# A two-layer RWKV-7 and differential-attention block: the parts of a recurrence step written first, its portions of other work behind them

## The chip, the cores and the metric

The kernel runs on one core of a Trainium2 chip. The time is device time in microseconds, the median of several runs; single runs of the kernel before lie between 2425.6 and 2431.77 us. The engines of the core are TensorE (PE), VectorE (DVE), ScalarE (ACT), GpSimd (POOL) and SyncE (SP), which here only issues DMAs. Each works through its own queue of instructions in order and waits at semaphores for the others.

## The reference

One sequence of 256 context tokens and 512 latent tokens (width 1024) goes through two layers. Each layer modulates a normalized input (adaLN), projects it, and mixes it in two ways: differential attention, and an RWKV-7 recurrence over 8 heads of 64, forward and backward. Then come the output projection and a squared-ReLU MLP. What matters here is the recurrence, and what is done with its result:

```python
def step(state, inp):
    r_t, w_t, k_t, v_t, kk_t, b_t = inp
    sa = jnp.einsum("bhvk,bhk->bhv", state, kk_t)
    state = (state * w_t[:, :, None, :] - sa[..., :, None] * b_t[:, :, None, :]
             + v_t[..., :, None] * k_t[:, :, None, :])
    y = jnp.einsum("bhvk,bhk->bhv", state, r_t)
    return state, y

for d, reverse in enumerate((False, True)):
    state_c, yc = wkv_scan(state0, rc, dec_c, km_c, vc, kkc, b_c, reverse)   # context first
    _, yl = wkv_scan(state_c, r, dec, km, v, kk, bb, reverse)                # then latents
    y_lat, y_ctx = y_lat + yl, y_ctx + yc
out = rwkv_finish(y_lat, ...)   # norm per head, bonus, gate
```

The modulation vectors are `silu(c) @ ada_w[l] + ada_b[l]`, six of width 1024 for each layer. Outputs of the context are not needed in the last layer.

## The kernel before

The recurrence works in chunks. A tile has 128 tokens, two chunks of 64; 6 tiles make the 768 tokens, in both directions d = 0 and 1 (d = 1 takes the tiles in another order). For each tile and direction **preparation** (`preps`, lines 962 to 1070) computes scaled keys and the products of keys with keys, G, in two halves of four heads. That needs a loading part (`prep_a`) and four more pieces (`prep_b`), so 5 portions for a half, 20 for both directions, and one more that reports the tile as ready. Then **inversion** (`inv`): blocks of G go to DRAM in another layout (`relay`, line 1086), come back (W and N, lines 1115 and 1116), are inverted by 30 pairs of instructions (`eliminate`, lines 1100 and 1102; on DVE from tile 2 on, on POOL for tiles 0 and 1), are stored (1123, 1127) and loaded back (1132, 1137), and `merge` joins the blocks with 64 small matmuls (1152 to 1162) and two copies (1164, 1165). An inversion has 11 portions.

A **step** (n, j) is chunk j of the n-th tile in both directions. It is a generator that yields after each part: X for d = 0 and 1 (lines 1186, 1189; evacuated by 1192), U (1198, 1201), the state (1210, 1213, 1215, 1218; left out in the last step) and Y (1226, 1236 or 1239; left out for the context in the last layer). That makes 8 parts, or 6. U of step (n, 0) is the first to need the merged G of tile n. After a tile's last Y, **finish** (lines 1244 to 1296, 3 portions) normalizes, gates and stores it for the output projection. **adaLN** (`ada_half`, line 265) streams its weights through three buffers of 512 KB on the SP queue; four pieces a step are drawn, and their loads are queued behind the last uv load of the step (`self.gate`, line 1176).

The order of instructions in each engine's queue is set when the kernel is built. A planner runs all instructions against its own estimate of their durations. When an engine is free in this estimate, it gets, of the instructions whose inputs the estimate holds ready, the one that is written earliest in the program. So the place in the program is a rank and not a fixed position. What the planner has laid down is the order on the chip, also where the real times differ from the estimate.

The loop that the change touches is in `rest()`. `work` holds finish portions, `ada` the adaLN pieces, `prepg` the preparation, `invs` the inversions; each call draws one portion.

```python
for _ in step(n, j):
    work(1)
    if nst == 0:
        with tc.issue_after(self.gate.ins):
            ada(ADA[l])
    nst += 1
    for _ in range(4):
        if n < 4 and n + 2 not in ready:
            next(prepg)
            ...
    invs(1)
```

Of the kernel before, what the change touches and what calls it, by code (L numbers as in the profile page):

```python
# [26 lines left out]
ADA = [4, 4]  # L27
# [137 lines left out]
class K:  # L165
# [760 lines left out]
    def recurrence(self, l, last, es, side):  # L926

        nc, tc, I, dr = self.nc, self.tc, self.I, self.dr
# [146 lines left out]
        def prep_until(n):  # L1075
            while n not in ready:
                next(prepg)
# [66 lines left out]
        def merge(n):  # L1144
            TT = tts.pop(n)
            Gs = [sets[(n, d)][2].rearrange("s u h t -> s (u h) t") for d in range(2)]
            a, e = slice(0, 32), slice(32, 64)
            get = late.get("pg", bank)
            zps = get([64, 16, 32])
            Z = iv.tile([64, 16, 32], F32, name=self.n("Z"), tag="Z")  # L1150
            for u in range(16):
                nc.tensor.matmul(zps[e, u, :], Gs[0][a, u, 32:64], TT[a, u, :],
                                 start=True, stop=True, skip_group_check=True)
                nc.tensor.matmul(zps[a, u, :], Gs[1][e, u, 0:32], TT[e, u, :],
                                 start=True, stop=True, skip_group_check=True)

            nc.scalar.copy(Z.rearrange("p u (i r) -> p u r i", r=2), zps.rearrange("p u (r i) -> p u r i", r=2))
            nps = get([64, 16, 32])
            for u in range(16):
                nc.tensor.matmul(nps[a, u, :], Z[e, u, :], Gs[0][e, u, 32:64],  # L1160
                                 start=True, stop=True, skip_group_check=True)
                nc.tensor.matmul(nps[e, u, :], Z[a, u, :], Gs[1][a, u, 0:32],
                                 start=True, stop=True, skip_group_check=True)
            nc.vector.tensor_copy(Gs[0][a, :, 32:64], nps[a])
            nc.scalar.copy(Gs[1][e, :, 0:32], nps[e])
# [138 lines left out]
        def rest():  # L1304
            nonlocal uvp, fp, px, us, xsd
            side.drain()
            setp.extend([self.pool(es, "sets", 1) for _ in range(2)])
            uvp = self.pool(es, "uvp", 2)
            xsd = [uvp.tile([128, 512], F32, name=self.n("xs"), bufs=1) for _ in range(2)]
            for x in xsd:  # L1310
                nc.gpsimd.memset(x[64:128], 0.0)
            fp = self.pool(es, "fp", 1)
            pg, pa, *px = (self.pool(es, "pg", 1, PSUM) for _ in range(4))
            late["pg"] = lambda shape: pg.tile(shape, F32, name=self.n("pg"), tag="g")
            us = self.pool(es, "pus", 1, PSUM).tile([128, 2, 4, 64], F32, name=self.n("us"))
            pms.append(self.pool(es, "pmr", 1, PSUM))
            ada = Fill()
            kinds = (("mix", "rows"), ("mlp", "cols"), ("mlp", "rows"))
            for kd, how in kinds:
                ada.add((self.ada_rows if how == "rows" else self.ada_cols)(l, kd, pa, "a"))  # L1320
            if l == 0:
                ada.add(self.ada_cols(1, "mix", pa, "a"))
            work = Fill()
            prep_until(1)
            invs = Fill()
            for n in range(6):
                if n == 0:
                    merge(0)
                    merge(1)
                for j in range(2):  # L1330
                    nst = 0
                    for _ in step(n, j):
                        work(1)
                        if nst == 0:
                            with tc.issue_after(self.gate.ins):
                                ada(ADA[l])
                        nst += 1

                        for _ in range(4):
                            if n < 4 and n + 2 not in ready:  # L1340
                                next(prepg)
                                if n + 2 in ready:

                                    invs.add(inv(n + 2))
                        invs(1)
                if n == 4:
                    invs.drain()
                while done:
                    work.add(finish(done.pop(0)))
            work.drain()  # L1350
            ada.drain()
            if l == self.dbg.get("layer", 0) and "orT" in self.dbg:
                for j in range(4):
                    nc.sync.dma_start(self.dbg["orT"][j], self.od[j])
# [385 lines left out]
```

## Time and profile before

| | us |
|---|---|
| median of 3 runs | 2428.95 |
| the profiled execution | 2426.55 |
| its span, first to last instruction | 2424.8 |
| PE busy | 2250.5 (93%) |
| DVE busy | 1518.5 (63%) |
| ACT busy | 1174.4 (48%) |
| POOL busy | 803.6 (33%) |

The busy time of PE is that of matmuls, which overlap in its pipeline. The granted clock is the share of full speed that PE is given. A busy share over the whole span is a mean over stages with different limits; the recurrence stands in the span twice, once for each layer, at about 490 to 760 us and 1757 to 2010 us.

### The profile page before, as it was taken

How to read it: one execution, taken by the hardware profiler on the slowest of the kernel's cores; microseconds unless marked ns; L12 is line 12 of the kernel's file. 1: busy time of each engine (PE TensorE's matmuls, PEld its weight loads, DVE VectorE, ACT ScalarE, POOL GpSimd, SP SyncE). 2: the span in 40 equal slices, each digit the busy share in tenths (PEclk: the TensorE clock that was granted, in tenths of full speed). 3: DMA queues.
4: the chain of work that ended last, by engine and by line, in shares of the span. 5: the costliest groups of instructions: out<-in, count | busy, mean ns of one | idle time of the engine just before them, and what ended most of it. 6: DMA issues, size and time to landing. Idle time of an engine off the chain costs nothing.

```text
span 2424.8 us, 43738 instructions
## 1 busy us (share of the span) xinstructions
PE 2250.5 (93%) x17150; PEld 1903.9 (79%) x17150; DVE 1518.5 (63%) x2629; ACT 1174.4 (48%) x2393; POOL 803.6 (33%) x1048
## 2 busy tenths in 40 slices
PE   6999998899988999999999999999879988999997
PEld 5887887787777988888888887778767877788886
DVE  5456458647755675555556736665856575778784
ACT  4345547545534544333344435555735544555552
POOL 1212324832212343333330422323562121553530
PEclk9999999779998999999999999999879988999999
DMA  7543445377577521111112344454567664423230
GB/s 275 157 131 87 122 126 134 81 207 186 148 190 221 196 92 60 64 61 62 61 63 85 136 137 133 115 144 110 115 171 198 153 181 161 165 88 121 86 114 35
DMA packets 291630, 313.67 MB, mean 129 GB/s; under 512 B 139680, under 2 KB 220896, under 8 KB 291424
## 3 DMA queue, kind: packets, MB, share of 16 engines
q1 hardware_dynamic: 280320, 284.66, 38.8%
q0 software_dynamic: 10240, 23.08, 5.0%
q8 instruction: 135, 2.21, 0.4%
q10 hardware_dynamic: 864, 3.15, 0.3%
q14 instruction: 71, 0.58, 0.1%
HBM read 257.04 MB, written 53.77 MB: 128 GB/s over the span
## 4 chain that ended last, share of the span: by engine, by line
PE 66%; DVE 10%; DMA 8%; issue 5%; POOL 4%; ACT 4%; SPq 2%; ACTq 0%; POOLq 0%; DVEq 0%
PE pf L351 32%; PE pu L351 16%; PE po L351 4%; DMA raw<-in_ada_w 2%; PE po L832 2%; PE pb L1046 2%; PE sc L795 1%; DVE wl L1500 1%; POOL pr L1100 1%; POOL W L1102 1%; PE X L1189 1%; DVE nm L797 1%; PE X L1226 1%; PE adar L265 1%; PE ptr L815 1%
## 5 line engine op out<-in xcount | busy, mean ns | idle before, releaser
L1500 DVE TENSOR_TENSOR wl<-raw,wh 128x1024 fp32r<-128x1024 f32 x170 | 255.8, 1507 | 125.0 <-ACT wh L1499 124.2
L351 PE MATMUL pf<-hl,wh 128*128 128x512 f32 (+1 forms) x832 | 282.1, 342 | 0.0
L351 PE MATMUL pf<-hh,wh 128*128 128x512 f32 (+1 forms) x832 | 280.5, 342 | 0.6 <-ACT hh L397 0.6
L351 PE MATMUL pf<-hh,wl 128*128 128x512 f32 (+1 forms) x832 | 275.7, 342 | 0.0
L1499 ACT ACTIVATE wh<-raw 128x1024 fp32r<-128x1024 f32 x170 | 179.2, 1058 | 161.5 <-PE pf L351 143.9
L351 PE MATMUL pf<-wh,fah 128*128 128x512 f32 x570 | 224.5, 396 | 13.2 <-DVE fu L1633 7.2
L351 PE MATMUL pu<-hh,wh 128*128 128x512 f32 (+1 forms) x632 | 223.7, 354 | 4.8 <-DVE t L557 1.7
L351 PE MATMUL pf<-wl,fah 128*128 128x512 f32 x570 | 223.9, 394 | 0.7 <-DVE wl L1500 0.7
L351 PE MATMUL pf<-wh,fal 128*128 128x512 f32 x570 | 221.4, 394 | 1.8 <-DVE fal L1600 1.8
L351 PE MATMUL pu<-hh,wl 128*128 128x512 f32 (+1 forms) x632 | 218.6, 346 | 4.0 <-DVE wl L340 4.0
L351 PE MATMUL pu<-hl,wh 128*128 128x512 f32 (+1 forms) x632 | 218.0, 345 | 0.0
L797 DVE TENSOR_REDUCE nm<-sc 128x1 f32<-128x768 f32 (+1 forms) x160 | 132.5, 841 | 79.3 <-PE sc L795 78.5
L351 PEld LDWEIGHTS pf<-hl,wh 128*128 128x128 f32 x832 | 156.6, 188 | 20.0 <-DVE hl L399 0.2
L351 PEld LDWEIGHTS pf<-hh,wl 128*128 128x128 f32 x832 | 156.1, 188 | 20.0
L351 PEld LDWEIGHTS pf<-hh,wh 128*128 128x128 f32 x832 | 155.3, 188 | 20.4 <-ACT hh L397 0.8
L799 ACT ACTIVATE e<-sc,nm 128x768 f32<-128x768 f32 (+1 forms) x160 | 130.7, 821 | 53.9 <-DVE nm L797 44.3
L321 POOL TENSOR_TENSOR rs<-ms,pw 128x1 f32<-128x1 f32 (+2 forms) x60 | 56.7, 948 | 271.2 <-DVE ms L319 270.5
L351 PEld LDWEIGHTS pu<-hh,wh 128*128 128x128 f32 x632 | 121.2, 192 | 23.4 <-DVE t L557 2.4
L351 PEld LDWEIGHTS pf<-wh,fah 128*128 128x128 f32 x570 | 107.2, 188 | 40.6 <-ACT fah L1599 13.6
L1633 DVE TENSOR_TENSOR acc<-pf,acc 128x512 f32<-128x512 f32 x155 | 104.2, 682 | 53.9 <-PE pf L351 53.3
L351 PEld LDWEIGHTS pu<-hh,wl 128*128 128x128 f32 x632 | 121.0, 192 | 19.0 <-DVE wl L340 4.8
L351 PEld LDWEIGHTS pu<-hl,wh 128*128 128x128 f32 x632 | 121.1, 192 | 14.3 <-issue 1.7
(262 smaller groups left out, 5607.1 us busy)
## 6 DMA issues: line engine op xcount, KB each, us to landing
raw<-in_w_ff SPq DMA_DIRECT2D x128, 512.0 KB, 3.7
raw<-in_ada_w SPq DMA_DIRECT2D x96, 512.0 KB, 6.5
raw<-in_w_in SPq DMA_DIRECT2D x52, 512.0 KB, 4.0
ld<-zd SPq DMA_DIRECT2D x40, 384.0 KB, 5.5
ks<-qd POOLq DMA_DIRECT2D x64, 192.0 KB, 5.4
zd<-zr SPq DMA_DIRECT2D x22, 384.0 KB
raw<-in_w_out SPq DMA_DIRECT2D x16, 512.0 KB, 5.9
qs<-qd POOLq DMA_DIRECT2D x32, 192.0 KB, 5.9
```

The source lines that it names most:

```text
L265: nc.tensor.matmul(acc[32 * g:32 * g + 32, :], self.sc[:, 2 * kp + k, :], raw[:, k, g * 128:g * 128 + 128], start=(kp + k == 0), stop=(kp ...
L321: nc.gpsimd.tensor_tensor(r, m, self.pw1.to_broadcast([128, cols]), ALU.pow)
L351: nc.tensor.matmul(out, a, b, start=(start and i == 0 and j == 0), stop=(i == n - 1 and j == 2), skip_group_check=not start)
L795: nc.tensor.matmul(sc[:, k0:k1], qs[:, br, tk], ks[:, br, k0:k1], start=True, stop=True)
L797: nc.vector.tensor_reduce(nm, sc, AX.X, ALU.max, negate=True)
L799: nc.scalar.activation(ee, sc, AF.Exp, bias=nm, accum_out=ls[:, br:br + 1])
L815: nc.tensor.transpose(pt[:, (k - k0) * 128:(k - k0) * 128 + 128], e[0][:, k * 128:k * 128 + 128], self.ident)
L832: nc.tensor.matmul(po, pT[:, k * 128:k * 128 + 128], vn[:, k, h * 64:h * 64 + 64], start=(k == 0), stop=(k == nk - 1))
L1046: nc.tensor.matmul(pgt[:, u, 0:nn], BK[hs, u, :], KR[hs, 2 * pp + u, 0:nn], start=True, stop=True, skip_group_check=True)
L1499: nc.scalar.activation(hi, src, AF.Copy)
L1500: nc.vector.tensor_tensor(lo, src, hi.bitcast(F32), sub)
L1633: nc.vector.tensor_tensor(d, p, d, add)
```

## The change

The step's generator is run to its end first, and its parts are counted. Then adaLN's pieces are drawn, and after them, once for every part, a finish portion, three portions of preparation instead of four, and an inversion portion. No instruction is added or taken away.

```diff
                 for j in range(2):
-                    nst = 0
-                    for _ in step(n, j):
+                    parts = sum(1 for _ in step(n, j))
+                    with tc.issue_after(self.gate.ins):
+                        ada(ADA[l])
+                    for _ in range(parts):
                         work(1)
-                        if nst == 0:
-                            with tc.issue_after(self.gate.ins):
-                                ada(ADA[l])
-                        nst += 1
-
-                        for _ in range(4):
+                        for _ in range(3):
                             if n < 4 and n + 2 not in ready:
                                 next(prepg)
                                 if n + 2 in ready:
                                     invs.add(inv(n + 2))
                         invs(1)
```

## Rows read from the trace of the kernel before

**Rows 1.** The page: busy time of PE, and its granted clock in 40 slices.

```profile
PE 2250.5 (93%) x17150; PEld 1903.9 (79%) x17150; DVE 1518.5 (63%) x2629; ACT 1174.4 (48%) x2393; POOL 803.6 (33%) x1048
...
PEclk9999999779998999999999999999879988999999
```

**Rows 2.** Windows: stretch, length, busy per engine (instructions), PEclk, DMA share, GB/s.

```profile
492.90:760.00 267.10, 245.18 (x3484) 198.03 (x3483) 170.84 (x462) 128.05 (x301) 65.50 (x112) 0.87 0.76 197
...
1757.00:2010.00 253.00, 227.12 (x3271) 188.85 (x3269) 159.81 (x439) 123.12 (x287) 77.11 (x171) 0.87 0.67 173
1757.00:1803.00 46.00, 33.65 (x464) 27.39 (x461) 19.66 (x45) 15.49 (x38) 31.34 (x82) 0.70 0.63 158
1847.00:1888.00 41.00, 39.66 (x520) 32.33 (x518) 31.53 (x99) 24.95 (x65) 9.19 (x22) 1.00 0.70 197
```

**Rows 3.** Groups by line, PE, 492.9 to 760: count, busy us, mean ns, idle before.

```profile
L265 PE MATMUL adar<-raw,sc 128*32 128x128 f32 x768 | 40.1, 301 | 14.4 <-DMA raw<-in_ada_w 13.6 <-DVE W L1102 0.6
```

**Rows 4.** Waits of PE in 490:740, then 1757:2010: us, times, longest.

```profile
PE adar L265 <- DMA raw<-in_ada_w: 13.6, 8, 2.8
...
PE us L1210 <- DVE st L1213: 8.5, 3, 5.2
```

**Rows 5.** Timeline of PE around step (4,1): start, us, instruction, [idle before].

```profile
702.10 1.39 PE L1186 MATMUL X<-uv,S 64*128 64x64 f32 x16
...
705.70 2.05 PE L1189 MATMUL X<-sbd,S 128*128 128x128 f32 x16
...
710.13 0.64 PE L265 MATMUL adar<-raw,sc 128*32 128x128 f32 x16 [1.71 <-DMA raw<-in_ada_w]
...
710.96 0.69 PE L1198 MATMUL us<-xs,S 128*64 128x64 f32 x16
711.48 0.98 PE L1226 MATMUL X<-uv,S 128*64 128x64 f32 x14
...
712.91 0.69 PE L1210 MATMUL us<-uv,S 128*64 128x64 f32 x16
```

**Rows 6.** Timeline of ACT, steps (4,1) and (5,0): first evacuation of X.

```profile
707.10 0.59 ACT L1192 ACTIVATE xs<-X 64x512 f32<-64x512 f32 x1
...
719.64 0.59 ACT L1192 ACTIVATE xs<-X 64x512 f32<-64x512 f32 x1 [0.27 <-PE X L1189]
```

**Rows 7.** Timeline of PE, DVE and ACT, 726 to 736: merge and U of (5,0).

```profile
726.84 0.22 PE L1162 MATMUL pg<-S,Z 32*32 32x32 f32 x2
...
732.08 2.08 PE L1281 MATMUL pb<-S,cst 128*128 128x512 f32 x2 [1.46 <-POOL S L1279]
...
735.09 1.12 PE L1198 MATMUL us<-xs,S 128*64 128x64 f32 x16
...
728.15 0.69 DVE L1282 TENSOR_TENSOR S<-pb,S 128x512 f32<-128x512 f32 x1 [5.25 <-DMA S<-zd]
...
729.36 0.67 DVE L1164 COPY S<-pg 32x512 f32<-32x512 f32 x1
...
730.66 1.50 ACT L1291 ACTIVATE S<-pb,pc 128x128 f32<-128x128 f32 x4 [2.53 <-PE pb L1288]
732.18 0.58 ACT L1165 COPY S<-pg 32x512 f32<-32x512 f32 x1
```

**Rows 8.** Timeline of PE, layer 1, ahead of U of (5,0).

```profile
1968.93 2.07 PE L1281 MATMUL pb<-S,cst 128*128 128x512 f32 x2
...
1978.32 2.07 PE L1281 MATMUL pb<-S,cst 128*128 128x512 f32 x2
...
1985.46 1.12 PE L1198 MATMUL us<-xs,S 128*64 128x64 f32 x16
```

**Rows 9.** Timeline of the SP queue, layer 1: the last load of N, tile 5.

```profile
1934.09 0.67 SPq L1116 DMA_DIRECT2D N<-da  x1
```

**Rows 10.** Timeline of DVE and PE, layer 1, step (0,0): eliminations and state.

```profile
1795.71 0.40 DVE L1100 TENSOR_TENSOR pr<-W,N 128x30 f32<-128x30 f32 x1 [3.15 <-DMA N<-da]
...
1800.09 1.12 PE L1210 MATMUL us<-uv,S 128*64 128x64 f32 x16 [5.20 <-DVE st L1213]
```

## The prediction

> **What bounds the kernel now.** I read the page first. Its engine line shows TensorE (PE) busy for 93% of the span; its slices show two regions in which the granted clock falls to 0.7 or 0.8 of full speed, slices 8 to 13 and 29 to 34 [rows 1]. The recurrence of layer 0 lies in the first, that of layer 1 in the second. The busy time by windows then gives each stage: 492.9 to 760 us and 1757 to 2010 us, together 520.1 us, with PE busy for 245.18 and 227.12 us, so idle for 21.9 and 25.9 us, and a mean granted clock of 0.87 in both [rows 2]. The clock has two levels, 2.4 and 1.2 GHz (shares 1.0 and 0.5); a mean of 0.87 is 26% of the time at the lower one, some 69 and 66 us, in which half as much gets done. All that a new order inside the recurrence can win is therefore about 48 us of idle time and about 67 us of clock. PE's work itself stays.
>
> Next, what PE does there. The groups by line show that the largest single line in layer 0 is not one of the step's products but the adaLN products, 768 with 40.1 us busy, laid between the parts [rows 3]. The list of waits says what ends PE's idle time: in layer 0 the adaLN weights, 13.6 us in 8 waits, the longest 2.8 us; in layer 1 an addition of the state on DVE, 8.5 us in 3 waits [rows 4]. A portion that waits holds the chain behind it, since each engine works in order.
>
> How long a step must be: in the full-clock rows around step (4,1) the products of one direction take 1.39 us (line 1186), half of 2.05 (1189), 0.69 (1198), 0.98 for 14 of 16, so 1.1 (1226), and 0.69 (1210): 4.9 us, 9.8 for both [rows 5]. From the first evacuation of X in this step, at 707.10, to that of the next, at 719.64, are 12.5 us [rows 6], with no preparation left to do. The 12 steps of layer 0 fill 267.1 us, 22 each. The difference is the portions' work, idle time and clock.
>
> **The change part by part.** No instruction is added or removed. What changes is the order of writing, which the planner reads as rank: of two instructions that its estimate holds ready, the earlier written one gets the engine. (a) All 6 to 8 parts of a step now outrank every portion written in that step; between steps the ranks stay. (b) Preparation goes on by 3 portions a turn instead of 4. A tile pair needs 21 (4 units of 1 + 4, and one more). With 4 a turn it is through in turn 6 of 8, with 3 in turn 7, so the inversion is begun one turn later; in layer 1, whose first four steps have 6 parts, 6 x 3 = 18 is short of 21, and it ends in the first turn of the next step. (c) adaLN, written behind the first part until now, is written behind the last. SP and POOL get the same instructions: the loads of adaLN stay behind the step's last uv load, and relay, N, W and finish loads are ranked behind both uv loads in either order.
>
> First term, adaLN. Its waits are real losses, because the step's products are queued behind them: at 710 us PE idles for 1.71 us before an adaLN product, and U of the second direction starts only at 710.96 [rows 5]. Written behind the step, an adaLN product is taken only where the planner holds no product of the step ready, hence later against its load. Bounds: nothing, and all of 13.6 us [rows 4]. The longest wait is 2.8 us; yielding to the X products of both directions alone, 2 x (1.39 + 1.03) = 4.8 us [rows 5], is more than that. I take three quarters, 10.2 us, and not all, because the first gap that the estimate leaves can still come before the load.
>
> Second term, the finish portions in step (5,0). In layer 0 the last two merge products start at 726.84 and end at 727.06, and U starts at 735.09. Between them the chain needs only the two copies of the merge, 0.67 us on DVE and 0.58 on ACT. But the DVE copy (729.36) stands behind a finish product that a load holds until 728.15; the ACT copy (732.18) behind four finish evacuations; U behind finish's matmuls of 2.08 us [rows 7]. 735.09 - 727.06 - 1.25 = 6.8 us are lost. Bounds 0 and 6.8; I take half, 3.4, since a finish instruction that the estimate holds ready while the merge is not goes first in either order. In layer 1 two finish products of 2.07 us stand among the products ahead of U of (5,0) [rows 8]: 4.1 us, half 2.1.
>
> Third term, against: preparation and inversion. Behind preparation of tile n+2 come relay to DRAM, load, 30 eliminations on DVE, stores and loads, merge, and only then U of step (n+2,0). In layer 1 the last load of N for tile 5 is issued at 1934.09 [rows 9], and U of (5,0) starts at 1985.46 [rows 8], 51 us later, with nothing but this sequence between; I find no slack there. If the preparation of tile 5 now yields to the whole step (3,0), it moves by at most 9.8 us [rows 5]; at least by nothing, since it is a chain of short instructions that fit into a step's gaps, and 12.5 - 9.8 = 2.7 us of them are there in a step with little else [rows 5, 6]. I take 4.8 us, the X products of both directions, after which the step first leaves PE a gap. For layer 0 I take nothing, since its U of (5,0) waits for finish as well (second term), and keep 9.8 as its bound.
>
> What is *not* gained: in layer 1 the eliminations of tile 2 run on DVE from 1795.71, ahead of the state's addition, and PE idles for 5.20 us until 1800.09 [rows 10]. They are written behind this step's parts in both kernels; the planner took them first because it held their load for done and U not yet. Rank doesn't mend that, and some portions will stand ahead in the new kernel too. (b) I cost at nothing for the tiles that have slack; without it, it is the third term again.
>
> Sum: -10.2 - 3.4 - 2.1 + 4.8 = -10.9 us against the profiled run's 2426.55, so 2415.7. The median of the runs shown, 2428.95, is 2.4 above that run: **2418 us**. By the bounds: all gains and no loss, -13.6 - 6.8 - 4.1 = -24.5, is 2404; no gain and 9.8 lost in each layer, +19.6, is 2449.
>
> **Rivals.** *Nothing to see.* PE is busy for 92% and 90% of these stages [rows 2]. An engine that is that full does the same work in any order, and from step to step the ranks are unchanged. For it: the 5.20 us at 1795, where rank did not decide. Against it: the finish instructions ahead of the merge. Time 2429, between 2423 and 2434 by terms that cancel.
>
> *Inversion late (slower).* One mechanism: preparation yields to the step, relay and elimination start later, and U of (n+2,0) waits for its merge. It decides from the point where that delay exceeds what the steps ahead of U save. Full price at one place in each layer, 2 x 9.8 = 19.6 [rows 5], with half of the adaLN gain, 6.8, against it: +12.8, so 2442. For it: no slack in layer 1 [rows 8, 9]. Against it: the choice by instruction, which lets portions into each gap.
>
> *Clock (slower).* The granted clock is low where PE waits: 0.70 in 1757 to 1803, where PE is busy for 33.65 of 46 us, against 1.00 in 1847 to 1888, where it is busy for 39.66 of 41 [rows 2]. If no portions lie between the parts, PE pauses in each step for the evacuations, and again in the run of portions behind it. A tenth of the two stages more at the lower level, 52 us, does the work of 26: +26, so 2455. The Trainium skill, "TensorE: Matmul & The Clock Gate", section "HAM oscillation", describes this: short groups of matmuls with waits between them lose the full clock again and again, so that by this rule taking the filler out of the waits is harmful. The two windows agree with it; that the gaps will open here no run shows yet.
>
> **How the numbers follow.** Measurement can tell about 0.3% from no change, 7.3 us: 2421.7 to 2436.2. The forecast's mechanism gets 0.50, with a range of its own of 2404 to 2427: 0.42 of it below 2421.7, 0.08 inside. Nothing to see gets 0.18; inversion late 0.22, 0.04 of it inside; clock 0.10. So faster 0.42, same 0.30, slower 0.28. For 8 in 10 the range goes from just under the bound of all gains, 2403, over the late inversion to 2446; above lie most cases of the clock.
>
> **What would show it.** Right: the adaLN waits of layer 0 under 6 us; less than 5 us from the last merge product to U of (5,0); the two stages shorter by about 11 us together. The third term: the N load of the last tile of layer 1 later against the end of step (2,1). Wrong: stages as long as now with their waits under other names; a mean clock under 0.87; U of (2,0) or (5,0) later than now with PE idle in front of it. A difference outside the two stages would speak against all of it.

## The result, and the profile after

The changed kernel takes 2466.49 us (median of 4 runs, 2453.88 to 2472.58) beside 2429.36 for the kernel before: a ratio of 1.013, 95% interval 1.0092 to 1.0167. It is slower by 37 us, and outside the predicted range. The profiled execution is the shortest of the four, 2453.88 us, with a span of 2452.1; against 2424.8 us before, 27 of the 37 us can be followed in the trace, and the rest cannot.

The page of the changed kernel, engine line, against [rows 1]:

```profile
PE 2256.2 (92%) x17150; PEld 1909.7 (78%) x17150; DVE 1515.9 (62%) x2629; ACT 1175.6 (48%) x2393; POOL 799.8 (33%) x1048
```

PE has the same 17150 matmuls and is busy for only 6 of the 27 us more; the rest is idle time. To place it I cut the span at U of (0,0), U of (2,0) and the last Y of each layer. From U of (2,0) to the last Y the steps use tiles 2 to 5, whose inversions are made inside the stage. The other five pieces come to -7.5, +2.9, -9.9, -2.8 and +8.8 us in their order, -8.5 in all. The windows of these two stretches (columns as in [rows 2]), first in the kernel before:

```profile
609.70:759.10 149.40, 133.83 (x2002) 107.45 (x2002) 94.62 (x267) 67.52 (x151) 32.37 (x38) 0.87 0.73 193
1871.60:2007.10 135.50, 126.77 (x1840) 107.07 (x1839) 88.89 (x247) 70.08 (x156) 26.08 (x40) 0.90 0.65 166
```

and in the changed kernel:

```profile
605.10:777.40 172.30, 142.81 (x2032) 116.39 (x2027) 98.33 (x270) 70.99 (x156) 28.81 (x38) 0.83 0.69 184
1877.20:2025.60 148.40, 129.93 (x1893) 109.25 (x1892) 99.15 (x289) 73.43 (x168) 26.48 (x44) 0.91 0.63 156
```

They are 22.9 and 12.9 us longer. PE's idle time (length less busy) grows from 15.6 to 29.5 and from 8.7 to 18.5 us. In layer 0 the granted clock falls from 0.87 to 0.83 besides: 39 us of 149.4 at 1.2 GHz before, 59 of 172.3 now; there PE is also busy for 9.0 us more, with 30 matmuls more inside the cuts. 22.9 + 12.9 - 8.5 is the 27.3 us of the spans.

What happens in layer 0 shows in the timelines of ACT, SP and PE around step (5,0), of the changed kernel:

```profile
714.24 0.57 ACT L1192 ACTIVATE xs<-X 64x512 f32<-64x512 f32 x1
...
667.89 0.86 SPq L1086 DMA_DIRECT2D da<-S  x2
669.41 1.29 SPq L1123 DMA_DIRECT2D dn<-W  x2
...
679.01 0.67 SPq L1116 DMA_DIRECT2D N<-da  x1
...
720.05 1.28 SPq L1123 DMA_DIRECT2D dn<-W  x2
721.37 4.04 SPq L1263 DMA_DIRECT2D S<-zd  x1
...
733.59 2.44 SPq L1137 DMA_DIRECT2D S<-dn  x2
...
733.25 1.08 PE L265 MATMUL adar<-raw,sc 128*32 128x128 f32 x16 [7.62 <-DMA raw<-in_ada_w]
...
749.10 0.24 PE L1162 MATMUL pg<-S,Z 32*32 32x32 f32 x1
752.06 1.12 PE L1198 MATMUL us<-xs,S 128*64 128x64 f32 x16 [2.73 <-DVE S L1164]
```

and on SP in the kernel before: the relay of tile 5, its last N load, the store behind its last pair and the first load back.

```profile
660.97 0.86 SPq L1086 DMA_DIRECT2D da<-S  x2
...
667.00 0.67 SPq L1116 DMA_DIRECT2D N<-da  x1
...
706.66 2.10 SPq L1123 DMA_DIRECT2D dn<-W  x2
...
716.62 1.05 SPq L1132 DMA_DIRECT2D TT<-dt  x2
```

The step gets what its new rank promises: X of (5,0) is evacuated at 714.24, 5.4 us sooner than before (719.64 in [rows 6]). But U starts 37.8 us behind that instead of 15.5, since the merge of tile 5 ends at 749.34 and not 727.06 [rows 7]. Its relay (667.89) is 7 us later than before, its last N load 12 us (SP puts the stores and loads of tile 4's inversion ahead of it, from 669.41), and behind the last pair the blocks stored at 720.05 are only begun to be fetched back at 733.59. That is 13.5 us later, where the kernel before took 10.0 (706.66 to 716.62). Between the two stand loads and output stores of finish, 9.7 us in all, and two adaLN loads, 0.8 us. The list of waits doesn't show this as a wait for the merge (2.7 us), because the planner had laid other work into the gap; the distance from X to U shows it.

In layer 1 the same happens at tile 3, in the timelines of ACT and PE: 21.4 us from X to U of (3,0), 4.1 before. First the changed kernel:

```profile
1913.96 0.59 ACT L1192 ACTIVATE xs<-X 64x512 f32<-64x512 f32 x1
...
1933.19 0.19 PE L1162 MATMUL pg<-S,Z 32*32 32x32 f32 x1
...
1935.40 0.69 PE L1198 MATMUL us<-xs,S 128*64 128x64 f32 x16
```

then the kernel before:

```profile
1905.70 0.59 ACT L1192 ACTIVATE xs<-X 64x512 f32<-64x512 f32 x1
...
1909.75 0.69 PE L1198 MATMUL us<-xs,S 128*64 128x64 f32 x16
```

The waits of PE, in 490:740 (layer 0) and 1757:2026 (layer 1), against [rows 4]:

```profile
PE adar L265 <- DMA raw<-in_ada_w: 17.2, 14, 7.6
...
PE us L1210 <- DVE st L1213: 9.4, 1, 9.4
```

adaLN waits more, not less. Its longest wait, 7.6 us, ends at 733.25, while the blocks of tile 5 are still to be fetched, so it held no product of the step up; without it 9.6 us are left. And the state's addition in layer 1 still stands behind eliminations, now for 9.4 us at once.

### The profile page after: what moved, and what is told of

It is laid out like the page before. It is cut to its first block, busy times and chain, and to the rows that moved or that the text cites. A ratio compares the mean times of both kernels' runs of the same rounds, so it can differ in the third digit from the quotient of the medians.

```text
span 2452.1 us, 43750 instructions
## 1 busy us (share of the span) xinstructions
PE 2256.2 (92%) x17150; PEld 1909.7 (78%) x17150; DVE 1515.9 (62%) x2629; ACT 1175.6 (48%) x2393; POOL 799.8 (33%) x1048
## 4 chain that ended last, share of the span: by engine, by line
PE 69%; DVE 9%; DMA 9%; ACT 4%; POOL 3%; issue 3%; SPq 2%; ACTq 0%; POOLq 0%; DVEq 0%
PE pf L351 32%; PE pu L351 15%; PE po L351 4%; DMA raw<-in_ada_w 3%; PE po L832 2%; PE pb L1046 2%; PE X L1186 2%; PE sc L795 1%; PE adar L265 1%; DVE wl L1498 1%; PE X L1189 1%; PE X L1226 1%; PE pb L977 1%; PE ptr L815 1%; POOL W L1102 1%
## 5 line engine op out<-in xcount | busy, mean ns | idle before, releaser
L351 PEld LDWEIGHTS pu<-hl,wh 128*128 128x128 f32 x632 | 121.8, 193 | 14.2 <-issue 1.7
```

Of the source, the lines that this page charges most:

```text
L351: nc.tensor.matmul(out, a, b, start=(start and i == 0 and j == 0), stop=(i == n - 1 and j == 2), skip_group_check=not start)
```

## The experiments

The theories: **A**, the loss goes through the inversion, which ends later against the step that needs it; within it, which of the moved portions makes it late. **B**, the smaller turn of preparation, 3 for 4. **C**, any other order is a worse draw of the planner's estimate against real times. **D**, adaLN's place. **K**, the clock: PE pauses in a step without portions, whatever the inversion does. **P** and **T** come with their runs: the queue of POOL, and the pace of preparation. In what follows a merge is called late when its last product ends behind the first evacuation of X of the step that needs it, and early when it ends ahead of it.

### One part of the change alone

The rank alone, with 4 portions of preparation a turn (a diff to the changed kernel):

```diff
-                        for _ in range(3):
+                        for _ in range(4):
```

> The changed kernel with four portions of preparation a turn instead of three: the new rank alone. If the inversions come late because the whole step outranks preparation (theory A), this stays slow: 2450 to 2470 us, with U of step (5,0) in layer 0 again 10 us or more later than before. If the smaller turn is the cause (theory B: in layer 1 the first steps have 6 parts, so 18 portions do not finish a tile's 21), most of the loss goes: 2425 to 2440 us, and the relay of tile 3 in layer 1 is back at its old distance from the start of the stage. If any new order is a draw of the planner's estimate against real times (theory C), it lands anywhere in 2420 to 2475 and the late inversions are not at the same tiles as in the changed kernel.

Measured: 2458.72 us, ratio 1.0105 (1.0064 to 1.0146). The turn of 3 alone, in the mixed order of before:

```diff
-                        for _ in range(4):
+                        for _ in range(3):
```

> The kernel before, with three portions of preparation after each part instead of four: the turn alone, parts and portions still mixed. Theory A (rank): within 0.5% of before, 2420 to 2440 us. Theory B (turn): slower, 2445 to 2470 us, and the loss is in layer 1, where tile 3 is ready later. Theory C (draw): anywhere in 2420 to 2475.

Measured: 2464.77 us, ratio 1.0137 (1.0102 to 1.0172). Each alone costs about as much as both together. So the costs don't add. That both use up the same margin is how I read it; the traces show merges that got much later than before in both, but at other tiles than in the changed kernel. There it was tile 5 of layer 0 and tile 3 of layer 1 (35.1 and 19.4 us late). With the rank alone it is tile 4 of layer 0 (14.6 us; tile 5 is early), with the turn alone tile 4 of layer 0 and tile 5 of layer 1 (22.2 and 20.9). That other tiles are late was the sign of C in the first expectation: A says by what the time is lost, but not at which tile.

The opposite rank, preparation and inversion ahead of the step:

```diff
-                    parts = sum(1 for _ in step(n, j))
+                    for _ in range(parts):
+                        for _ in range(4):
+                            if n < 4 and n + 2 not in ready:
+                                next(prepg)
...
+                        invs(1)
+                    for _ in step(n, j):
+                        pass
                     with tc.issue_after(self.gate.ins):
                         ada(ADA[l])
                     for _ in range(parts):
                         work(1)
```

> The opposite rank: in each turn preparation (four at a time) and inversion are written ahead of the whole step, adaLN and finish behind it. Theory A: preparation and inversion are the longer path, so this is faster than the changed kernel by at least 20 us and at or below before, 2405 to 2435 us; U of step (5,0) in layer 0 starts at 735 us or earlier. Theory B gives the same as for a turn of four, 2425 to 2440. Theory C: anywhere in 2420 to 2475.

Measured: 2461.33 us, ratio 1.0125 (1.0072 to 1.0179). It is slower too, but by another way. From U of (2,0) to the last Y, layer 0 takes 152.1 us, as before; layer 1 is slow at a low clock, while its merges are in time (that of tile 5 ends at 1984.9, X of (5,0) is evacuated at 2010.6). Layer 1's window of this kernel, and a piece of it:

```profile
1753.00:2035.00 282.00, 243.32 (x3196) 200.47 (x3186) 164.28 (x437) 121.76 (x285) 78.60 (x176) 0.77 0.60 149
...
1893.00:1923.00 30.00, 30.00 (x321) 25.96 (x321) 21.94 (x71) 13.46 (x33) 4.34 (x11) 0.57 0.39 100
```

243.32 us busy at 0.77 where before had 227.12 at 0.87 in its stage [rows 2]. The low clock is shown, and K expects it. That missing portions cause it is argued: the clock falls in a pause (from 1888 to 1896 PE is busy for 5.35 of 8 us), but then it is low while PE is busy without a gap. Preparation and inversion may go too early as well as too late.

adaLN behind the step, everything else mixed as before, in both layers and in layer 0 only:

```diff
                     for _ in step(n, j):
                         work(1)
-                        if nst == 0:
-                            with tc.issue_after(self.gate.ins):
-                                ada(ADA[l])
...
+                    with tc.issue_after(self.gate.ins):
+                        ada(ADA[l])
```

> The kernel before with one edit: the adaLN pieces are drawn behind the whole step and its portions, parts and portions still mixed. My prediction said that writing adaLN behind the step saves about 10 us of PE's waits for its weights: 2415 to 2425 us if that holds. If adaLN's place is instead what costs (theory D: its loads come in bunches between the inversion's DMAs), 2440 to 2465 us. Theory A and B: no change, 2420 to 2438.

> Layer 0 with adaLN's four pieces drawn behind the step and its portions (as in the run that did so in both layers), layer 1 in the order of before; parts and other portions mixed as before in both. In the run for both layers, layer 0 was 11 us shorter than before and layer 1 23 us longer. Theory D (the place of adaLN in layer 0 is what can be gained, and layer 1's loss comes from its own order): 2412 to 2422, faster than before by 0.3 to 0.7%. Theory C (layer 1's length depends on where the planner happens to stand when it starts): layer 1 comes out as no one can say, 2415 to 2445.

Measured: 2442.01 us, ratio 1.0041 (1.0011 to 1.0071), and 2442.68, ratio 1.0047 (1.0023 to 1.0071). In both profiles layer 0 is some 10 us shorter from its first U to its last Y (247 and 249 us for 257), and layer 1 longer by more. That this is the size of the predicted first term is in part luck: the waits for adaLN weights fall from 13.6 to 8.6 and 8.1 us, half of it, and the merge of tile 5 is 18 and 16 us early there, where before has it 7.4 late. In the second kernel the text of layer 1 is that of before; the planner goes on from where layer 0 left it. Why layer 1 then loses is not settled.

### The inversion taken out

The 30 pairs of elimination left out for tiles 2 to 5, once in the order of before and once in the new order:

```diff
             for t in range(1, 31):
                 k, w = (t + 1) // 2, 31 - t
+                if n < 2:
...
+                    ve.tensor_tensor(W[:, 0:k, t + 1:32], W[:, 0:k, t + 1:32], prv, ALU.add)
-                ve.tensor_tensor(W[:, 0:k, t + 1:32], W[:, 0:k, t + 1:32], prv, ALU.add)
                 if t % 4 == 0:
                     yield
```

> The order of before, with the 30 pairs of elimination left out for tiles 2 to 5 in both layers (loads, stores, transfers and merge stay; what comes out of the inversion is then wrong). It takes 35 to 40 us of DVE chain out of every inversion. Theory A (the time that the new order costs comes from the inversion, which is late against U): before has little lateness left to lose in layer 0 (12.7 us from the last merge product, and 9 us of it finish's), somewhat more in layer 1, so 2405 to 2425. Theory C (each order is a draw of estimate against real times): could come out on either side, 2410 to 2450. The kernel is read against its twin, the new order without the pairs.

> The new order with the same 30 pairs left out for tiles 2 to 5 (what comes out of the inversion is then wrong). Theory A: the inversion then ends some 35 us earlier, which is more than the 17 to 25 us that U of (5,0) and (3,0) wait for the merge in the changed kernel; the waits go, and with them the whole difference: within 8 us of its twin in the old order, or below it. Theory K (the clock: without portions between the parts PE pauses in every step, and the lower clock follows, whether the inversion is late or not): 15 to 30 us above the twin, with some 30 us more at half clock. Theory C: the difference to the twin is of any sign, and the idle time lies at other places than in front of U.

Measured: 2411.52 us in the old order (ratio 0.9924, 0.99 to 0.9948), 2417.5 in the new (0.9946, 0.992 to 0.9972). Of 37 us of difference 6 are left, and the intervals overlap. The same two windows as above, of the old order without the pairs:

```profile
590.80:742.30 151.50, 138.88 (x2050) 112.30 (x2049) 67.58 (x128) 75.18 (x174) 35.31 (x46) 0.93 0.80 215
1846.60:1976.90 130.30, 119.69 (x1828) 101.84 (x1822) 55.41 (x105) 66.90 (x154) 23.08 (x36) 0.92 0.63 163
```

and of the new:

```profile
588.70:745.60 156.90, 142.52 (x2081) 116.86 (x2079) 64.42 (x123) 72.84 (x172) 33.70 (x47) 0.87 0.71 191
1872.20:1997.80 125.60, 116.84 (x1813) 99.53 (x1812) 54.87 (x103) 65.60 (x147) 25.64 (x37) 0.93 0.70 178
```

281.8 and 282.5 us: in these stretches, with a short inversion, the order of writing is worth nothing, in either direction. The whole spans of the two traces differ more, 2403.2 and 2416.8 us: the piece between the layers is 18 us longer in the new order, though the change has no line there. That stays unexplained. Without the pairs every merge of tiles 2 to 5 is 14 us or more early, in both orders; in the new order tile 5 of layer 0, by the timelines of PE and ACT:

```profile
700.50 0.24 PE L1163 MATMUL pg<-S,Z 32*32 32x32 f32 x1
...
723.83 0.59 ACT L1193 ACTIVATE xs<-X 64x512 f32<-64x512 f32 x1
...
725.28 0.69 PE L1199 MATMUL us<-xs,S 128*64 128x64 f32 x16
```

U follows X by 1.5 us where it took 37.8. This shows A, and speaks against K as the main cause: the same ranks cost little once the inversion is short. The edit also frees DVE, where the state's additions stand behind the pairs; but in the two stretches PE waits for the state on DVE for only 1.0 us in the changed kernel and 3.1 before, so the longer stretches of the changed kernel are not that wait. What K may keep is in layer 0, where the clock is 0.87 for 0.93 and the stretch 5.4 us longer; layer 1 gives 4.7 of it back.

### The same work on another engine

All eliminations on POOL, in both orders; and only those of tiles 3 and 5:

```diff
-                ve = nc.gpsimd if n < 2 else nc.vector
+                ve = nc.gpsimd
```

> The order of before, with the eliminations of all tiles on POOL instead of those of tiles 0 and 1 alone. In the profiled run of before one pair takes 0.38 + 0.40 us on POOL, so 30 pairs 23 us; on DVE they have 0.26 + 0.26 us each, 16 us of work, but stand between other instructions and take 23 to 54 us from first to last. POOL is busy for 65 and 77 us of the two stages. Theory A (what an order costs here is how far the inversion's end lies behind the step that needs it): a shorter inversion gives before some of the 17 us that leaving the pairs out gave: 2412 to 2426. Rival P (POOL's own queue is in order too, and preparation's instructions on POOL then stand behind the pairs; the two engines also slow each other): as long as before or longer, 2429 to 2445.

> The new order with the eliminations of all tiles on POOL. Theory A: the inversion's chain of 30 pairs goes from 23 to 39 us down to about 23 and no longer stands between the state's additions on DVE; the 17 to 25 us that U of (5,0) and of (3,0) wait for the merge shrink by some 10 each, and the time comes to 2425 to 2445; the difference to its twin in the old order is about half of the 31 us seen with the pairs on DVE, 8 to 20 us. Theory C (a draw of estimate against real times): the difference to the twin is of any sign. Rival P: 2455 or more, the inversion is as late as on DVE.

> The order of before, with the eliminations of tiles 3 and 5 on POOL too, those of 2 and 4 still on DVE, so that two inversions that follow each other use two engines. Theory A: part of what the twin with all tiles on POOL gives, 2415 to 2428. Rival P: no gain, 2429 to 2445. Theory C: 2420 to 2450, the layers each of a length that nothing in the edit explains.

Measured: 2444.12 us (1.0036, 1.001 to 1.0062) in the old order, 2459.33 (1.0105, 1.0063 to 1.0147) in the new, and 2434.72 (1.0002, 0.9975 to 1.0029) with tiles 3 and 5. The difference between the orders, 15 us, is half of that on DVE, and A had named 8 to 20; but A's reason for it does not hold, since the inversion is hardly shorter: a pair takes 0.38 + 0.39 us on POOL (medians), and from the last N load to the store of tile 2 are 46 us in layer 0, 47 before. Nothing is won against before, as P expected. In the new order merges are late here too, with DVE free of the pairs: tiles 2, 3 and 5 of layer 0 by 15.9, 15.9 and 13.5 us.

### A harmless change of rank, and the pace of preparation

finish drawn last in each turn, and preparation by 5 and by 7 portions a turn, all in the mixed order of before:

```diff
                     for _ in step(n, j):
-                        work(1)
...
                         invs(1)
+                        work(1)
```

> Before with one harmless change of rank: in each turn the finish portion is drawn last, behind the preparation and inversion portions, and not first. The first finish portions are there only after (2,1) in layer 0, and finish has slack but for the last tiles. Theory A alone (only what delays the inversion costs): the inversion goes a little ahead of finish, so the same time or a little less, 2420 to 2432. Theory C (the layers' lengths are draws, and that of layer 1 of before, as short as without the pairs, is a lucky one): layer 1 comes out at 255 to 285 us instead of 247, and the time at 2435 to 2460, though nothing that the inversion waits for was moved behind anything.

```diff
-                        for _ in range(4):
+                        for _ in range(5):
```

> Before, with preparation by 5 portions a turn instead of 4 (by 3 it came to 2465). Theory A (what counts is how soon behind X of (n,0) the preparation of tile n+2 ends, and with it how late its merge is): preparation is through in turn 5 of 8 instead of 6, the inversion begins a turn earlier, and the time is that of before or a little under it, 2415 to 2432. Rival T (a step's own products are what then yields, and 4 is the middle between two losses): 2435 to 2460, with the steps stretched and merges early.

> Before, with preparation by 7 portions a turn, so that it is through in turn 3. Theory A: merges are all early against U of their step, 2410 to 2430. Rival T: the stages get longer, since U and the state stand behind preparation's products; 2440 to 2465, with more time at half clock as in the run with preparation ahead of the step (2461).

Measured: 2432.37 us (1.0004, 0.9977 to 1.0031); 2432.16 (0.9991, 0.9959 to 1.0024); 2436.84 (1.0036, 1.0005 to 1.0067). C in its strong form falls: two other orders give the time of before. With 3, 4, 5 and 7 portions a turn the ratios are 1.0137, 1, 0.9991 and 1.0036. From 3 to 4 the time drops by 1.4%, with 5 nothing more is won, and with 7 there is a small loss, the way that T names but less than its range.

### Parts of the change undone

In the changed kernel, the inversion's portions alone ahead of the step; preparation alone ahead; adaLN alone back behind the first part; and the last two together:

```diff
-                    parts = sum(1 for _ in step(n, j))
+                    parts = 6 if last and n < 2 or n == 5 and j == 1 else 8
+                    invs(parts)
+                    for _ in step(n, j):
+                        pass
...
-                        invs(1)
```

> The new order with one part undone: the inversion's portions are drawn ahead of the step instead of behind it, so that they outrank the step's parts; preparation (3 a turn), adaLN and finish stay behind the step. Theory A in its narrow form (it is the inversion's own instructions that yield to the step): U of (5,0) in layer 0 and of (3,0) in layer 1 no longer wait 17 to 25 us for the merge, and 20 us or more come back: 2425 to 2440. Theory A in its wide form (preparation yields, the inversion only follows): little comes back, 2445 to 2460. Theory C: 2440 to 2470, with waits at other steps.

```diff
+                    for _ in range(3 * parts):
+                        if n < 4 and n + 2 not in ready:
+                            next(prepg)
...
+                    for _ in step(n, j):
+                        pass
...
-                        for _ in range(3):
-                            if n < 4 and n + 2 not in ready:
-                                next(prepg)
...
```

> The new order with preparation alone (3 portions a turn) put ahead of the step; adaLN, finish and inversion stay behind it, as in the changed kernel. Theory A in its wide form (preparation that yields to the step is what makes the merges late; the inversion's own rank costs nothing, as the run with the inversion alone ahead showed): from U of (2,0) to the last Y, layer 0 comes from 172 us back to about 150, and the merge of tile 5 ahead of X of (5,0). For layer 1 the run with preparation and inversion ahead says 155 to 160 by the clock. In all 2440 to 2460. If layer 0 stays at 165 to 175 us, preparation's rank is not the cause.

```diff
-                    parts = sum(1 for _ in step(n, j))
-                    with tc.issue_after(self.gate.ins):
-                        ada(ADA[l])
+                    parts = 0
+                    for _ in step(n, j):
+                        if parts == 0:
+                            with tc.issue_after(self.gate.ins):
+                                ada(ADA[l])
+                        parts += 1
```

> The new order with adaLN's pieces drawn behind the first part of the step, where before had them, and all other portions behind the step. Theory A: adaLN has no part in the loss, so the time stays at 2455 to 2470, with U of (5,0) in layer 0 as late against its X as in the changed kernel (38 us). Theory D (adaLN's loads and products behind the step are what collides with the inversion's end: the wait of 7.6 us for its weights at 718 to 726): 2435 to 2450.

> The new order with two of its moves undone: preparation (3 portions a turn) ahead of the step, adaLN behind the step's first part. Only finish and inversion stay behind the whole step. Each of the two alone gave back about half of the loss (ratios 1.006 and 1.005 against 1.013). Theory A with D (the two delay the same merges, and one that is in time again brings nothing more): 2435 to 2450, hardly under the single ones. If they add up: 2425 to 2436, the time of before. Rival K (clock): 2450 or more, with layer 1 at half clock for 110 us or longer, as in the other runs with preparation ahead.

And the changed kernel again, on the chip of the last one:

> The changed kernel itself, unedited, beside the run with two of its moves undone on the same chip, so that their difference is read there and not over several chips. If what undoing adaLN gave back (16 us in medians) is real, this one stands at 1.010 to 1.017 again, 2457 to 2475; if the first measurement of it was a high draw, at 1.004 to 1.009.

Measured: inversion ahead 2456.02 us, ratio 1.0106 (1.0071 to 1.0141); preparation ahead 2451.66, 1.0062 (1.0023 to 1.0101); adaLN back 2449.77, 1.0054 (1.0025 to 1.0082); both 2440.12, 1.0024 (0.9989 to 1.0059); the changed kernel again 2465.15, 1.0142 (1.0066 to 1.0219), with U of (5,0) at 750.11 and X at 714.32, as in its first trace.

So the inversion's own rank is not the cause: with it undone, X to U of (5,0) still takes 36.2 us in layer 0. Preparation's rank and adaLN's place are: by the ratios each undone gives back about half (for preparation the interval touches that of the changed kernel), both together 25 us of 31 on the same chip. Whether the two add up is not settled: 2440.12 us lies in the range named for delays that do not add (2435 to 2450), the ratio rather speaks for adding, and the intervals overlap. The trace with both undone has no merge of tiles 2 to 5 more than 2.1 us late, and the two stretches take 154.6 and 142.1 us, together 296.7, where the changed kernel has 320.7 and the one before 284.9.

The one trace of preparation alone ahead is that of its longest execution, 2470.14 us, so no lengths are read from it.

How preparation acts, in the timelines of ACT and SP: from X of (3,0), the step in which tile 5 is prepared, to the last relay of tile 5 in layer 0. The changed kernel's relay, 667.89, and that of before, 660.97, are shown above. X of the changed kernel:

```profile
644.91 0.59 ACT L1192 ACTIVATE xs<-X 64x512 f32<-64x512 f32 x1
```

before:

```profile
648.63 0.59 ACT L1192 ACTIVATE xs<-X 64x512 f32<-64x512 f32 x1
```

both undone:

```profile
638.08 0.58 ACT L1192 ACTIVATE xs<-X 64x512 f32<-64x512 f32 x1
...
652.67 0.83 SPq L1086 DMA_DIRECT2D da<-S  x2
```

23.0, 12.3 and 14.6 us. For tile 4, behind X of (2,0), it is 45.3, 26.6 and 10.4 us; but 6.1 us of the 45.3 the finished relay stands on SP behind the stores and loads of tile 3's inversion, and tile 4's merge is no later than before for it (3.0 us late, 5.0 before).

How adaLN acts is not shown as clearly. This is the SP queue behind the elimination of tile 5, in the kernel with adaLN alone back:

```profile
716.92 1.24 SPq L1123 DMA_DIRECT2D dn<-W  x2
...
721.10 0.92 SPq L1132 DMA_DIRECT2D TT<-dt  x2
722.12 3.15 SPq L1137 DMA_DIRECT2D S<-dn  x4
```

5.2 us from the store to the first load of the blocks (L1137), where the changed kernel took 13.5 and the one before 11.1 (706.66 to 717.72). From the store to the last merge product are 15.5 us instead of 29.1 (20.2 before). But in the changed kernel adaLN's own loads were only 0.8 of those 13.5 us; finish's loads and stores filled most of the rest, and why they came to stand elsewhere is not shown. In this profile the chain then waits at tile 4 instead (19.2 us from X to U), and layer 0 is no shorter (174.5 us from U of (2,0) to the last Y, 172.3 in the changed kernel). The 16 us that its median gives back are measured, but by which path, and where they lie in the runs without a trace, stays open. Nor are late merges the whole of a stage's length: here tile 4 is the worst, 18.3 us late, while the kernel with preparation and inversion ahead has two merges of layer 0 late by 15.6 and 13.9 us and takes 152.1.

## Why the prediction was wrong

**The third term** is the step that failed most: it put the lateness of the inversion at 4.8 us, with 9.8, PE's own time for a step, as the most, and it counted preparation alone. Preparation did yield, and the size was too small: its last product G, on DVE, comes 2.9 to 14.5 us later than before behind X of the step that prepares the tile (tiles 2 to 5 of both layers), in four of the eight cases more than 9.8. A step lasts some 20 us, not 9.8, and preparation is a chain over five engines, each of which can make it wait. But more than half of the lateness arose behind preparation, where the term put nothing. For tile 5 of layer 0, counted from X of (3,0), the relay is 10.7 us later than before, the last N load 15.7, the store behind the last pair 17.1 and the end of the merge 26.0. For tile 3 of layer 1, counted from X of (1,0), the relay is 3.5 us later, the end of the elimination 11.0 (its pairs take 37.7 us instead of 31.0) and the end of the merge 17.2. In place of +4.8, U came 22.4 us later behind X at (5,0) in layer 0 and 17.4 at (3,0) in layer 1; of the latter 8.9 us are X coming sooner, which gains nothing when U has to wait.

**Layer 0 at nothing** failed with it. The argument was that U of (5,0) waits for finish as well. But the merge came 22 us later, and U followed its last product by 2.7 us: finish was not what it waited for.

**(b) at nothing** failed outright: the turn of 3 alone costs 1.4%. Tiles were said to have slack; without the pairs the merges are 14 us or more early, with them those of layer 0 (tiles 2 to 5) are 4.0 to 14.2 us *late* even in the kernel before. That was to be read beforehand: [rows 6] and [rows 7] have X at 719.64 and the merge at 727.06.

**First term, adaLN: -10.2.** It failed in the changed kernel: 17.2 us of waits instead of under 6. Its step "taken only where the planner holds no product ready, hence later against its load" counted the products alone. The weight loads are written with them and moved behind the step as well. That they stay behind the last uv load was right; that the move costs nothing elsewhere was the error: undone, it gives back some 16 us. That this goes over the SP queue, where these loads share the order with the stores and loads of an inversion, is argued and not shown. With the other portions mixed, layer 0 did win some 10 us, half of it in these waits, and layer 1 lost them.

**Second term, finish.** Its test held and was worth nothing: from the last merge product to U are 2.7 us (8.0 before), under the 5 that were named, but the merge itself was late.

**What is not gained** was right: the state's addition behind eliminations, 9.42 us for 5.20 [rows 10].

**The rivals.** *Inversion late* had the right mechanism, with a chance of 0.22, and the wrong price: 2 x 9.8 less an adaLN gain that did not come. The two stretches in which it acts grew by 35.8 us in the profile, 23.7 of them idle time of PE and 12.1 busy time. *Clock* is not what decides here; it shows in layer 0 (0.83 for 0.87, and without the pairs 0.87 for 0.93), not in the stretch of layer 1 (0.91 for 0.90), and most in layer 1 of the run with preparation and inversion ahead. There the rule that the prediction cites from the Trainium skill, "TensorE: Matmul & The Clock Gate", section "HAM oscillation", agrees with the trace in part: the clock falls in a pause of PE, as the rule has it (5.35 of 8 us busy from 1888 to 1896), but it is 0.57 in the 30 us from 1893 in which PE is busy throughout, and no run shows that portions between the parts would have kept it up. In the new order without the pairs the same portions stand behind the step, and the clock is 0.93 in layer 1. *Nothing to see* was wrong for this kernel, and right for its recurrence without the pairs.

Of the named signs, "U of (5,0) later than now with PE idle in front of it" came true (with 2.73 us idle, since other work filled the gap), and so did longer stages and a mean clock under 0.87 (0.86 from 485 to 778 us, 0.84 from 1753 to 2026); the N load of the last tile in layer 1 was the wrong place to look: there tile 3 was late, and tile 5 had 14 us to spare. The prediction also said that a difference outside the two stages would speak against all of it. There are two, -9.9 us between the layers and +8.8 behind the second, and no mechanism told here explains them.

## What to carry to other kernels

Before portions of a side chain are moved behind the main one, measure for every place where they meet how long the side chain's result comes ahead of its need; where it is nothing or negative already, a later rank costs time, however full the engine is. Follow the side chain to its end and count what each of its links can lose, in the DMA queue as well, where loads and stores of other work may come to stand between its own. The time that one engine is busy in a step is no upper bound for a yield (14.5 us for 9.8 here). And where a side chain decides, shorten it first: here the order of writing was then worth nothing inside the recurrence.

## What was not expected of the hardware

Leaving out 240 pairs takes 112 us off DVE's busy time (1406.6 us for 1518.5 [rows 1]), and only 17 us off the kernel. With the order of every queue fixed, the kernel before spreads over 2412.52 to 2450.19 us in 31 runs on one chip, and the kernel with adaLN back over 2437.43 to 2459.04 in 10, so a difference of 10 us between two single traces says little.
